# A decoder trunk's head: unused products in TensorE's pauses, x transposed between conditioning bursts, a second job's loads moved ahead

## The chip, the cores and the metric

The kernel runs on one core of a Trainium2 chip. The metric is the device time of one launch in microseconds (us). TensorE (PE in the profile; PEld is its weight load) multiplies and transposes into PSUM, VectorE (DVE), ScalarE (ACT) and GpSimd (POOL) work elementwise, and SyncE (SP) issues most of the transfers.

## What is computed

One layer of a decoder trunk, for a prompt of 256 tokens and for 8 samples of 8 tokens, which share all weights. In the reference (cut):

```python
mod = jax.nn.silu(c) @ w_ada + b_ada
sh1, sc1, g1, sh2, sc2, g2 = jnp.split(mod, 6, axis=-1)
h = _rmsnorm(x, norm1_g) * (1 + sc1) + sh1
p = h @ w_in                      # q, k, v, og, u, ga, gb, alr
o, s_new = _gla(q, k, v, loga, s0)
y_a = _rmsnorm(o, gla_norm_g) * silu(og);  y_b = _pool(u_ext, pos0, w_pool, pool_scale)
x = x + g1 * ((sigmoid(ga) * y_a + sigmoid(gb) * y_b) @ w_o)
h2 = _rmsnorm(x, norm2_g) * (1 + sc2) + sh2
gate, up = jnp.split(h2 @ w_gu, 2, axis=-1)
x = x + g2 * ((silu(gate) * up) @ w_down)
```

x is (320, 2048), c is (9, 2048): one row for the prompt, one for each sample; w_ada is 2048 x 12288, w_in 2048 x 11280. All is float32.

## The kernel before

All activations lie transposed in SBUF: 128 channels on the partitions, the 320 tokens along the free dimension (`TP` 256 of the prompt, then 64 of the samples). The 2048 channels are 16 column blocks, k = 0 to 15.

**Exact products in three.** A piece of weights (`raw`) comes by a transfer that SyncE issues; ScalarE rounds it to `whi` (L152), VectorE takes the rest, `wlo` (L153), and each 128x128 block takes three products in a row (`mm3`, L166 to L168): hh by whi, hl by whi, hh by wlo, where hh and hl are the same split of h. `raw` has three buffers, so the fourth piece of w_in waits until the first has been split.

**The head** (the pool `head`, from the loads of c and x on) prepares h. c is transposed (16 small transposes), its silu goes to `scT`. x comes in three row blocks `xn`; for every column block k three transposes (128, 128 and 64 rows) go into one buffer of the small PSUM pool (`misc`, four buffers), and VectorE or ScalarE copies them out to `xT[k]` (L462). Then the transposes of the bias and gain vectors (`bada`, `vec`), the sums of squares on ScalarE (L476), their square root behind a table load (L477), the reciprocal (L478) and three diagonal matrices `dg` (L483), with which three products (L484) spread 1/rms over all partitions: `rx`.

**Conditioning in jobs.** The modulation is made in slices of column blocks, `SLICES = ((0, 2), (2, 4), (4, 8), (8, 12), (12, 16))`. A `HeadJob` for a slice loads pieces of w_ada (eight buffers, `araw`), multiplies them with scT in bursts over four or two channel blocks (L218; 32 products on TensorE for a job of two blocks), and `finish` copies the sum (L438), transposes it (L129) and adds bias and gain (L233, L236) into `mod`. `h_unit(k)` then makes hh[k] and hl[k] (L490 to L499). The first job runs alone in the head; the job of the next slice is spread between the products of the slice before it.

**Slices of w_in.** For each slice, 15 units (q, k, v in two halves, u, og, ga, gb, and four gb units of other heads) multiply their 256 columns of w_in over the slice's two or four blocks into `pmain` (two PSUM buffers of two banks), and are copied or added out (`evac`, L338 to L355). The slices of two blocks take v, og, ga and gb in pairs (`proj_pair`).

**What sets the order.** The order of instructions on each engine is settled when the kernel is built: a scheduler ranks them by their place in the code and by what they wait for, and an instruction that is handed to `tc.keep_in_program_order` keeps its place among the others so marked on its engine. SyncE issues its transfers in the order of the code and waits in that order for free buffers.

Of the kernel before, what the change touches and what calls it, by code (L numbers as in the profile page):

```python
# [80 lines left out]
def body(tc, A):  # L81
# [74 lines left out]
    def split_chunk(src, nk, nn):  # L156
# [13 lines left out]
    def proj(w, col, k0, k1, xh, xl):  # L170

        ps = pmain.tile([P, 2, 512], F32, tag="pm", name=nm("ps"))
        for c0 in range(k0, k1, 4):
            nk = min(4, k1 - c0)
            for j, whi, wlo in split_chunk(w[:, c0:c0 + nk, col:col + 256], nk, 256):
# [21 lines left out]
    def proj_pair(w, col, k0, k1, xh, xl):  # L197

        parts = list(split_chunk(w[:, k0:k1, col:col + 512], k1 - k0, 512))
# [179 lines left out]
    with tc.tile_pool(name="head", bufs=1) as xp:  # L379
# [17 lines left out]
        nc.gpsimd.dma_start(vr1[64:68, :], A["gla_norm_g"][0].rearrange("(r p) -> r p", p=P))  # L397
        pt = misc()
# [4 lines left out]
        S.activation(csig, crT, AF.Sigmoid)  # L403
# [5 lines left out]
        class HeadJob:  # L409
# [25 lines left out]
            def finish(self):  # L435
                nb = self.s // 2
                sb = xp.tile([P, 2 * P], F32, tag="adasb", name=nm("adasb"))
                S.copy(sb[:, 0:self.w], self.ps[:, 0:self.w])  # L438
                pt = misc()
                for c in range(nb):  # L440
                    tr(pt[:, c * P:(c + 1) * P], sb[:, c * P:(c + 1) * P])
# [11 lines left out]
        for k in range(KT):  # L453
# [4 lines left out]
            if k < SLICES[0][1]:  # L458
                xT.append(xp.tile([P, T], F32, name="xT%d" % k))
            else:  # L460
                xT.append(hp.tile([P, T], F32, tag="hl%d" % k, name="xT%d" % k))
            (S.copy if k % 2 else V.tensor_copy)(xT[k], pt[:, 0:T])  # L462

        pt = misc()
# [7 lines left out]
        ssq = xp.tile([P, 3], F32, name="ssq")  # L472
        V.memset(ssq, 1.0)
        for i in range(3):
            n = P if i < 2 else TS
            S.activation(junk[:n], xn[i][:n], AF.Square, accum_out=ssq[:n, i:i + 1])  # L476
# [3 lines left out]
        dg = xp.tile([P, 3, P], F32, name="dg")  # L480
        for i in range(3):
            n = P if i < 2 else TS
            V.tensor_scalar(dg[:n, i, :n], ident[:n, :n], ssq[:n, i:i + 1], None, op0=ALU.mult)  # L483
            PE.matmul(prs[:, i * P:i * P + n], lhsT=ones[:n, :], rhs=dg[:n, i, :n], start=True, stop=True)  # L484
        rx = xp.tile([P, T], F32, name="rx")
        V.tensor_copy(rx, prs[:, 0:T])
# [42 lines left out]
        for f in HeadJob(0, SLICES[0][1]).steps():  # L529
            f()  # L530
        for k in range(SLICES[0][1]):
            h_unit(k)
        for si, (k0, k1) in enumerate(SLICES):
            bg = []
            acc = 0 if si == 0 else 1
            if si + 1 < len(SLICES):
# [5 lines left out]
                bg += HeadJob(n0, n1 - n0).steps()  # L542
# [673 lines left out]
```

## Time and profile before

| | |
|---|---|
| time of the kernel before, median of 3 runs | 1988.42 us (1988.23 to 1989.18) |
| the profiled execution's own time | 1986.94 us |
| its span from the first to the last instruction | 1985.1 us |
| TensorE busy, mean granted clock over the span | 98%, 0.993 |
| VectorE, ScalarE, GpSimd busy | 51%, 41%, 7% |
| transfers | 400.84 MB, mean 202 GB/s |

Times within the profile count from the span's start; the span is 1.8 us shorter than the execution's own time. A matmul's duration contains its way through the array, so successive products overlap, and their spacing is what a product costs.

### The profile page before, as it was taken

What the parts mean: (1) busy time and instruction counts of PE and PEld (TensorE: products, weight loads), DVE (VectorE), ACT (ScalarE), POOL (GpSimd) and SP (SyncE); (2) the same over time, 40 slices, a digit from 0 to 9 for tenths busy, and PEclk for the clock granted to TensorE, in tenths of its full rate; (3) what the DMA queues carried; (4) which work ended last, traced back from release to release, by engine and by line L of the source; (5) the groups of instructions that cost most, each with busy time, mean ns of one, the idle gap of its engine ahead of it and who ended that gap; (6) DMA issues with size and microseconds to landing.
All of it is one profiled execution on the core that took longest, in us unless ns stands there. A gap on an engine that the chain in (4) does not pass through costs nothing.

```text
span 1985.1 us, 37225 instructions
## 1 busy us (share of the span) xinstructions
PE 1943.5 (98%) x15030; PEld 1850.1 (93%) x15030; DVE 1012.2 (51%) x1888; ACT 818.8 (41%) x1470; POOL 135.6 (7%) x259
## 2 busy tenths in 40 slices
PE   7999999999999999999999999999999999999997
PEld 5789998898999899888999999999999999999997
DVE  2556565474546544664474434444444444444554
ACT  4333374354336433643354333333333434344443
POOL 1112220111010100110030000000000000000000
PEclk9999999999999999999999999999999999999998
DMA  9888754775975787579656666444445444444443
GB/s 299 288 303 271 228 168 141 266 267 181 329 249 167 279 273 232 168 252 331 223 156 219 198 217 195 142 153 146 151 145 159 149 149 149 150 151 146 149 141 93
DMA packets 324607, 400.84 MB, mean 202 GB/s; under 512 B 13545, under 2 KB 264681, under 8 KB 324097
## 3 DMA queue, kind: packets, MB, share of 16 engines
q1 hardware_dynamic: 312162, 358.21, 56.2%
q0 software_dynamic: 12272, 40.25, 5.5%
q8 instruction: 118, 1.93, 0.4%
q14 instruction: 55, 0.45, 0.1%
HBM read 373.96 MB, written 24.67 MB: 201 GB/s over the span
## 4 chain that ended last, share of the span: by engine, by line
PE 91%; DMA 5%; DVE 2%; ACT 1%; issue 0%; SPq 0%; DVEq 0%; ACTq 0%
PE ps L166 27%; PE ps L168 26%; PE ps L167 26%; PE pm L218 4%; DMA raw<-w_in 2%; PE pm L129 2%; DMA raw<-w_ada 1%; DMA raw<-w_o 1%; PE pm L804 1%; PE pm L825 1%; PE pm L773 1%; DVE wlo L153 1%; DMA xn<-x_sample 1%; DMA x<-xspill 0%; PE pm L800 0%
## 5 line engine op out<-in xcount | busy, mean ns | idle before, releaser
L153 DVE TENSOR_TENSOR wlo<-raw,whi 128x512 fp32r<-128x512 f32 x953 | 658.8, 696 | 813.1 <-ACT whi L152 809.9
L152 ACT CAST whi<-raw 128x512 fp32r<-128x512 f32 x953 | 586.2, 621 | 987.0 <-PE ps L167 825.8
L166 PE MATMUL ps<-hh,whi 128*128 128x320 f32 x1408 | 443.2, 315 | 6.0 <-ACT hh L495 2.7
L168 PE MATMUL ps<-hh,wlo 128*128 128x320 f32 x1408 | 440.3, 313 | 0.4 <-DVE wlo L153 0.2
L167 PE MATMUL ps<-hl,whi 128*128 128x320 f32 x1408 | 438.6, 312 | 0.3 <-DVE hl L499 0.3
L166 PE MATMUL ps<-h2h,whi 128*128 128x320 f32 x1408 | 437.3, 311 | 1.4 <-ACT h2h L1100 1.4
L167 PE MATMUL ps<-h2l,whi 128*128 128x320 f32 x1408 | 436.2, 310 | 0.5 <-DVE h2l L1086 0.5
L168 PE MATMUL ps<-h2h,wlo 128*128 128x320 f32 x1408 | 436.0, 310 | 0.0
L166 PEld LDWEIGHTS ps<-hh,whi 128*128 128x128 f32 x1408 | 265.3, 188 | 24.9 <-issue 10.5
L168 PEld LDWEIGHTS ps<-hh,wlo 128*128 128x128 f32 x1408 | 265.5, 189 | 8.6 <-issue 5.7
L167 PEld LDWEIGHTS ps<-hl,whi 128*128 128x128 f32 x1408 | 265.6, 189 | 7.5 <-issue 5.9
L166 PEld LDWEIGHTS ps<-h2h,whi 128*128 128x128 f32 x1408 | 265.0, 188 | 3.8 <-issue 2.2
L167 PEld LDWEIGHTS ps<-h2l,whi 128*128 128x128 f32 x1408 | 265.3, 188 | 0.9 <-DVE h2l L1086 0.9
L168 PEld LDWEIGHTS ps<-h2h,wlo 128*128 128x128 f32 x1408 | 265.2, 188 | 0.0
L166 PE MATMUL ps<-ah,whi 128*128 128x320 f32 x704 | 218.5, 310 | 0.0
L168 PE MATMUL ps<-ah,wlo 128*128 128x320 f32 x704 | 217.7, 309 | 0.0
L167 PE MATMUL ps<-al,whi 128*128 128x320 f32 x704 | 217.6, 309 | 0.0
L167 PEld LDWEIGHTS ps<-al,whi 128*128 128x128 f32 x704 | 132.2, 188 | 0.0
L166 PEld LDWEIGHTS ps<-ah,whi 128*128 128x128 f32 x704 | 132.2, 188 | 0.0
L168 PEld LDWEIGHTS ps<-ah,wlo 128*128 128x128 f32 x704 | 132.1, 188 | 0.0
L218 PE MATMUL pm<-raw,scT 128*32 128x128 f32 (+1 forms) x2688 | 103.0, 293 | 4.7 <-DMA raw<-w_ada 4.7
L218 PEld LDWEIGHTS pm<-raw,scT 128*32 128x32 f32 x2688 | 70.7, 110 | 25.5 <-issue 13.8
(292 smaller groups left out, 1540.2 us busy)
## 6 DMA issues: line engine op xcount, KB each, us to landing
raw<-w_ada SPq DMA_DIRECT2D x192, 512.0 KB, 6.1
raw<-w_gu SPq DMA_DIRECT2D x176, 512.0 KB, 3.5
raw<-w_in SPq DMA_DIRECT2D x173, 512.0 KB, 4.4
raw<-w_down SPq DMA_DIRECT2D x79, 512.0 KB, 3.3
S<-state_gla POOLq DMA_DIRECT2D x16, 1024.0 KB, 8.5
o_gs<-S POOLq DMA_DIRECT2D x16, 1024.0 KB, 7.6
raw<-w_o SPq DMA_DIRECT2D x32, 512.0 KB, 5.1
raw<-w_down SPq DMA_DIRECT2D x15, 256.0 KB, 2.6
```

Of the source, the lines that this page charges most:

```text
L129: PE.transpose(out, in_, ident[:k, :k])
L152: S.copy(hi, raw)
L153: V.tensor_sub(lo, raw, hi.bitcast(F32))
L166: PE.matmul(ps, lhsT=whi, rhs=xhi, start=start, stop=False)
L167: PE.matmul(ps, lhsT=whi, rhs=xlo, start=False, stop=False)
L168: PE.matmul(ps, lhsT=wlo, rhs=xhi, start=False, stop=stop)
L218: ins = PE.matmul(ps[32 * j:32 * j + 32, 0:w], lhsT=scT[:, k, :], rhs=raws[j], start=k == 0 if start is None else start, stop=k == KT - 1 ...
L773: PE.matmul(pt, lhsT=E["kdn"][:, s, d * P:(d + 1) * P], rhs=E["vn"][:, s], start=s == 0, stop=s == 1)
L804: PE.matmul(pt[32 * j:32 * j + 32, :], lhsT=qeP[:, d, 4 * gg + j, :], rhs=E["S0", gg, d][:, j], start=False, stop=d == 1, tile_position=(0 ...
L825: PE.matmul(pt, lhsT=kpz[:, gg, j, d * P:(d + 1) * P], rhs=E["vp"][:, gg], start=True, stop=True)
```

## The change

**Unused products.** A tile `fill` (128x512, ones) is made by four copies on VectorE, and `keep_busy(n)` multiplies it n times into a PSUM buffer that nobody reads. It is called with 6 ahead of c's transposes, 3 behind them; 9, 6 and 3 behind the transposes of x's first, second and third row block; 4 after the transposes behind each of the first three bursts; 1 before and 6 after `finish`.

**x between bursts.** Only column blocks 0 to 2 are transposed as x's row blocks land. The other 13 follow in program order behind the first job's bursts: 4, 5, 4 and none. The sums of squares come ahead of that, and the norm (`x_norm`) ahead of the third burst; it also leaves the normalized x of blocks 0 and 1 ready, to which `h_first` applies the modulation.

**Loads and splits.** The second job's first four pieces of w_ada (`job1.load(0)`, `job1.load(4)`) are issued ahead of w_in's fourth piece (unit u). The splits of w_in's first four pieces (`EarlySplit`) and `h_first` stand in one fixed order on ScalarE and VectorE.

The core of the diff:

```diff
+    class EarlySplit:
...
+        def hi(self):
+            tc.keep_in_program_order(S.copy(self.h, self.raw))
+
+        def lo(self):
+            tc.keep_in_program_order(V.tensor_sub(self.l, self.raw, self.h.bitcast(F32)))
...
+        def keep_busy(n):
+
+            for _ in range(n):
+                tc.keep_in_program_order(PE.matmul(idle[:, 0, :], lhsT=fill[:, 0:P], rhs=fill, start=True, stop=True))
...
+        keep_busy(6)
         pt = misc()
         for k in range(KT):
-            tr(pt[:, 16 * k:16 * k + 9], crow[:, k * P:(k + 1) * P])
+            ptr(pt[:, 16 * k:16 * k + 9], crow[:, k * P:(k + 1) * P])
+        keep_busy(3)
...
+        def x_trans(k, eng):
             pt = misc()
             for i in range(3):
                 n = P if i < 2 else TS
-                tr(pt[:, i * P:i * P + n], xn[i][:n, k * P:(k + 1) * P])
...
+                ptr(pt[:, i * P:i * P + n], xn[i][:n, k * P:(k + 1) * P])
+            xT.append(x_place(k))
+            (S.copy if eng else V.tensor_copy)(xT[k], pt[:, 0:T])
+
+        job0 = HeadJob(0, SLICES[0][1])
+        for k0 in range(0, KT, 4):
+            job0.load(k0)
...
+        for i in range(3):
+            n = P if i < 2 else TS
+            S.activation(junk[:n], xn[i][:n], AF.Square, accum_out=ssq[:n, i:i + 1])
+        pts = [misc() for _ in range(NX0)]
+        for i in range(3):
+            n = P if i < 2 else TS
+            for k in range(NX0):
+                ptr(pts[k][:, i * P:i * P + n], xn[i][:n, k * P:(k + 1) * P])
+            keep_busy((9, 6, 3)[i])
+        for k in range(NX0):
+            xT.append(x_place(k))
+            V.tensor_copy(xT[k], pts[k][:, 0:T])
...
+        def x_norm():
+            dg = xp.tile([P, 3, P], F32, name="dg")
+            for i in range(3):
+                n = P if i < 2 else TS
+                V.tensor_scalar(dg[:n, i, :n], ident[:n, :n], ssq[:n, i:i + 1], None, op0=ALU.mult)
+                tc.keep_in_program_order(PE.matmul(prs[:, i * P:i * P + n], lhsT=ones[:n, :], rhs=dg[:n, i, :n],
+                                                   start=True, stop=True))
+            V.tensor_copy(rx, prs[:, 0:T])
+            for k in range(SLICES[0][1]):
+                t = xp.tile([P, T], F32, tag="xh", bufs=2, name=nm("xh"))
+                V.tensor_tensor(t, xT[k], rx, op=ALU.mult)
+                xhat.append(t)
+
+        def h_first(k):
+
+            t = xhat[k]
+            E = G if k else V
+            pinned(S.activation(hh[k][:, 0:TP], t[:, 0:TP], AF.Identity, scale=modp(1, k), bias=modp(0, k)))
+            pinned(E.tensor_tensor(s3(t[:, TP:T]), s3(t[:, TP:T]), mods(1, k), op=ALU.mult))
+            pinned(E.tensor_tensor(s3(t[:, TP:T]), s3(t[:, TP:T]), mods(0, k), op=ALU.add))
+            pinned(S.copy(hh[k][:, TP:T], t[:, TP:T]))
+            hl[k] = hp.tile([P, T], F32R, tag="hl%d" % k, name="hl%d" % k)
+            pinned(V.tensor_scalar(t[:, 0:TP], t[:, 0:TP], modp(1, k), modp(0, k), op0=ALU.mult, op1=ALU.add))
+            pinned(V.tensor_sub(hl[k], t, hh[k].bitcast(F32)))
...
-        for f in HeadJob(0, SLICES[0][1]).steps():
-            f()
-        for k in range(SLICES[0][1]):
-            h_unit(k)
+        nx = SLICES[0][1]
+        for i, k0 in enumerate(range(0, KT, 4)):
+            if i == 2:
+                x_norm()
+            job0.burst(k0)
+            while len(xT) < (7, 12, 16, 16)[i]:
+                x_trans(len(xT), len(xT) % 2)
+            if i < 3:
+                keep_busy(4)
+        ew = []
+        job1 = HeadJob(nx, SLICES[1][1] - nx)
+        for kind, i, col in units(0)[:5]:
+            if kind == "v" and i == 1:
+                continue
+            if kind == "u":
+                job1.load(0)
+                job1.load(4)
+            raw = raw_chunk(win[:, 0:nx, col:col + (512 if kind == "v" else 256)], nx, 512 if kind == "v" else 256)
+            ready[col] = [EarlySplit(raw)] if kind != "v" else [EarlySplit(raw[:, j:j + 1]) for j in range(nx)]
+            ew += ready[col]
+        keep_busy(1)
+        job0.finish()
+        keep_busy(6)
+        ew[0].hi()
+        h_first(0)
+        ew[0].lo()
+        ew[1].hi()
+        h_first(1)
+        ew[1].lo()
+        for e in ew[2:]:
+            e.hi()
+            e.lo()
```

Where the instructions stand. VectorE, from the silu of c on, before (pm_159 and the like are x's transposes in PSUM, one for each column block):

```order
L404 TENSOR_TENSOR scT<-pm_139,csig 128x16x9
L462 COPY xT_163<-pm_159 128x320
L462 COPY xT_175<-pm_171 128x320
L462 COPY xT_187<-pm_183 128x320
L462 COPY xT_199<-pm_195 128x320
L478 RECIPROCAL ssq<-ssq 128x3
L483 TENSOR_SCALAR dg<-cst,ssq 128x128 x2
L483 TENSOR_SCALAR dg<-cst,ssq 64x64
```

And the same engine and place in the changed kernel (pm_195, pm_196 and pm_197 are column blocks 0 to 2):

```order
L445 TENSOR_TENSOR scT<-pm_151,csig 128x16x9
L538 RECIPROCAL ssq<-ssq 128x3
L547 TENSOR_SCALAR dg<-cst,ssq 128x128 x2
L547 TENSOR_SCALAR dg<-cst,ssq 64x64
L528 COPY xT_225<-pm_195 128x320
L528 COPY xT_227<-pm_196 128x320
L528 COPY xT_229<-pm_197 128x320
```

The reciprocal and dg, which wait for ScalarE's square root, now stand ahead of the first copy of x; four copies stood ahead of them.

TensorE in the changed kernel, from x's second row block to burst 0 (pm_247 is the first job's sum, pm_231 the vectors' transposes; in brackets the semaphores that a row waits for, of which DVE_49 is VectorE's):

```order
L431 MATMUL idle_139<-fill 128x512 x6
L435 MATMUL pm_195<-cst,xn_122 128x64 [waits DMAHW4_49]
L435 MATMUL pm_196<-cst,xn_122 128x64
L435 MATMUL pm_197<-cst,xn_122 128x64
L431 MATMUL idle_139<-fill 128x512 x3
L129 MATMUL pm_231<-cst,vr_133 128x68 [waits DMASW4_49,DMASW3_49,DMASW5_49,DMASW2_49,DMASW1_49]
L242 MATMUL pm_247<-raw_174,scT 32x128 [waits DMAHW5_49,DVE_49]
L242 MATMUL pm_247<-raw_174,scT 32x128
```

Burst 0 (pm_247) stood behind all transposes of x and the norm; now it stands behind those of three column blocks, and the other blocks follow it.

SyncE's queue before, from w_in's first piece on (raw_393 to raw_479 of w_in are the pieces of q, k, v and u):

```order
L142 DMA raw_393<-w_in 128x2x256
L142 DMA raw_413<-w_in 128x2x256
L142 DMA raw_436<-w_in 128x2x512
L142 DMA raw_474<-w_ada 128x4x256
L142 DMA raw_476<-w_ada 128x4x256
L142 DMA raw_479<-w_in 128x2x256
```

And in the changed kernel:

```order
L142 DMA raw_414<-w_in 128x2x256
L142 DMA raw_418<-w_in 128x2x256
L142 DMA raw_422<-w_in 128x2x512
L142 DMA raw_428<-w_ada 128x4x256
L142 DMA raw_430<-w_ada 128x4x256
L142 DMA raw_432<-w_ada 128x4x256
L142 DMA raw_434<-w_ada 128x4x256
L142 DMA raw_436<-w_in 128x2x256
```

Two more pieces of the second job stand ahead of u's.

## Rows read from the trace of the kernel before

**Rows 1.** Page, part 1: busy us, share of the span, instructions, by engine.
```profile
PE 1943.5 (98%) x15030; PEld 1850.1 (93%) x15030; DVE 1012.2 (51%) x1888; ACT 818.8 (41%) x1470; POOL 135.6 (7%) x259
```

**Rows 2.** Busy time by stretch; columns: from:to, length, then as its header says.
```profile
core 0: us, PE busy (x) PEld busy (x) DVE busy (x) ACT busy (x) POOL busy (x), PEclk, DMA share, GB/s
13.71:24.67 10.96, 10.96 (x36) 5.64 (x36) 4.02 (x11) 5.46 (x11) 0.00 (x0) 1.00 1.10 350
...
34.86:40.59 5.73, 5.40 (x24) 4.75 (x25) 2.12 (x6) 1.85 (x5) 3.24 (x7) 0.70 1.05 333
...
50.00:75.00 25.00, 25.00 (x252) 23.07 (x251) 16.07 (x29) 10.78 (x21) 5.11 (x10) 1.00 0.79 258
75.00:95.00 20.00, 17.22 (x155) 12.61 (x152) 8.13 (x13) 4.15 (x8) 0.00 (x0) 1.00 1.00 363
```

**Rows 3.** Chain of waits, 26 to 41 us; columns: start, length, engine, tile, line.
```profile
29.99 1.52 PE pm L218 x48
...
32.51 0.19 DVE mod L236
...
40.59 0.41 PE ps L166
```

**Rows 4.** Timeline of ScalarE, 12.9 to 33.2; start, length, operation.
```profile
14.85 1.22 ACT L462 COPY xT<-pm 128x320 f32<-128x320 f32 x3
16.09 1.28 ACT L477 ACT_TABLE_LOAD   x1
17.39 0.30 ACT L477 ACTIVATE ssq<-ssq,epst 128x3 f32<-128x3 f32 x1
```

**Rows 5.** Timeline of VectorE, 13 to 36.5.
```profile
17.71 0.18 DVE L478 RECIPROCAL ssq<-ssq 128x3 f32<-128x3 f32 x1 [0.66 <-ACT ssq L477]
18.00 0.64 DVE L483 TENSOR_SCALAR dg<-cst,ssq 128x128 f32<-128x128 f32 x3
18.56 0.48 DVE L462 COPY xT<-pm 128x320 f32<-128x320 f32 x1
...
33.57 1.51 DVE L153 TENSOR_TENSOR wlo<-raw,whi 128x512 fp32r<-128x512 f32 x2
...
35.68 0.47 DVE L497 SCALAR_TENSOR_TENSOR hl<-xh,mod,hh 128x256 fp32r<-128x256 f32 x1
```

**Rows 6.** Transposes by line L129: ns min/median/max, first and last start us.
```profile
L129 PE MATMUL pm<-cst,w x56: 270/272/415, 324.9 to 822.1; 128*128 128x128 f32 x56
...
L129 PE MATMUL pm<-cst,xn x48: 311/418/477, 6.8 to 24.4; 128*128 128x128 f32 x32, 64*128 64x64 f32 x16
```

**Rows 7.** Timeline of TensorE, 6 to 39.3.
```profile
24.89 1.73 PE L484 MATMUL pm<-dg,cst 128*128 128x128 f32 x6
...
34.86 0.68 PE L166 MATMUL ps<-hh,whi 128*128 128x320 f32 x2 [2.68 <-ACT hh L495]
...
36.77 0.47 PE L167 MATMUL ps<-hl,whi 128*128 128x320 f32 x1
37.04 0.47 PE L168 MATMUL ps<-hh,wlo 128*128 128x320 f32 x1
...
38.90 0.31 PE L167 MATMUL ps<-hl,whi 128*128 128x320 f32 x1
39.05 0.31 PE L168 MATMUL ps<-hh,wlo 128*128 128x320 f32 x1
```

**Rows 8.** Conditioning products of the first job, line L218, columns as in rows 6.
```profile
L218 PE MATMUL pm<-raw,scT x128: 272/273/421, 26.6 to 31.2; 128*32 128x128 f32 x128
```

**Rows 9.** Busy time from 26 to 30 us, columns as in rows 2.
```profile
26.00:30.00 4.00, 4.00 (x88) 3.48 (x91) 0.49 (x1) 0.38 (x1) 0.32 (x1) 1.00 0.18 51
```

**Rows 10.** Page, part 6: DMA issues, count, KB each, median us to landing.
```profile
raw<-w_in SPq DMA_DIRECT2D x173, 512.0 KB, 4.4
```

**Rows 11.** Busy time of three later stretches, columns as in rows 2.
```profile
612.00:615.10 3.10, 3.10 (x27) 3.09 (x27) 2.73 (x10) 1.31 (x3) 0.00 (x0) 1.00 0.23 41
275.00:280.00 5.00, 3.64 (x24) 3.18 (x22) 3.15 (x5) 4.97 (x9) 1.55 (x1) 1.00 0.21 71
280.00:285.00 5.00, 4.98 (x21) 4.77 (x22) 3.56 (x6) 4.90 (x9) 0.09 (x1) 0.66 0.68 195
```

More of the change, by code (lines that the diff above doesn't have):

```diff
@@ L154, in split, with __init__, split_chunk @@
         return hi, lo
-    def split_chunk(src, nk, nn):
+    ready = {}
+    class EarlySplit:
+        def __init__(self, raw):
+            n = raw.shape[2]
+            self.raw = raw
+            self.h = wp.tile([P, 512 // n, n], F32R, tag="whi", bufs=WB, name=nm("whi"))
+            self.l = wp.tile([P, 512 // n, n], F32R, tag="wlo", bufs=WB, name=nm("wlo"))
+        def hi(self):
+            tc.keep_in_program_order(S.copy(self.h, self.raw))
+        def lo(self):
+            tc.keep_in_program_order(V.tensor_sub(self.l, self.raw, self.h.bitcast(F32)))
+    def split_chunk(src, nk, nn, key=None):
+        if key in ready:
+            k = 0
+            for e in ready.pop(key):
+                for j in range(e.h.shape[1]):
+                    yield k, e.h[:, j], e.l[:, j]
+                    k += 1
+            return
         raw = raw_chunk(src, nk, nn)
@@ L174, in proj @@
             nk = min(4, k1 - c0)
-            for j, whi, wlo in split_chunk(w[:, c0:c0 + nk, col:col + 256], nk, 256):
+            for j, whi, wlo in split_chunk(w[:, c0:c0 + nk, col:col + 256], nk, 256, col if w is win else None):
                 kt = c0 + j
@@ L397, in body, with ptr @@
         nc.gpsimd.dma_start(vr1[64:68, :], A["gla_norm_g"][0].rearrange("(r p) -> r p", p=P))
+        idle = pmain.tile([P, 2, 512], F32, tag="pm", name=nm("idle"))
+        fill = xp.tile([P, 512], F32R, name="fill")
+        V.tensor_copy(fill[:, 0:P], ones)
+        for c in range(1, 4):
+            V.tensor_copy(fill[:, c * P:(c + 1) * P], ones)
+        def keep_busy(n):
+            for _ in range(n):
+                tc.keep_in_program_order(PE.matmul(idle[:, 0, :], lhsT=fill[:, 0:P], rhs=fill, start=True, stop=True))
+        def ptr(out, in_):
+            k = in_.shape[0]
+            tc.keep_in_program_order(PE.transpose(out, in_, ident[:k, :k]))
+        keep_busy(6)
         pt = misc()
         for k in range(KT):
-            tr(pt[:, 16 * k:16 * k + 9], crow[:, k * P:(k + 1) * P])
+            ptr(pt[:, 16 * k:16 * k + 9], crow[:, k * P:(k + 1) * P])
+        keep_busy(3)
         csig = xp.tile([P, KT, 9], F32, name="csig")
         crT = pt[:, 0:256].rearrange("p (k r) -> p k r", r=16)[:, :, 0:9]
-        S.activation(csig, crT, AF.Sigmoid)
+        tc.keep_in_program_order(S.activation(csig, crT, AF.Sigmoid))
         V.tensor_tensor(scT[:, :, 0:9], crT, csig, op=ALU.mult)
@@ L437, in finish @@
                 sb = xp.tile([P, 2 * P], F32, tag="adasb", name=nm("adasb"))
-                S.copy(sb[:, 0:self.w], self.ps[:, 0:self.w])
+                ins = S.copy(sb[:, 0:self.w], self.ps[:, 0:self.w])
+                if self.b0 == 0:
+                    pinned(ins)
                 pt = misc()
                 for c in range(nb):
-                    tr(pt[:, c * P:(c + 1) * P], sb[:, c * P:(c + 1) * P])
+                    (tr if self.b0 else ptr)(pt[:, c * P:(c + 1) * P], sb[:, c * P:(c + 1) * P])
                 src = pt[:, 0:nb * P].rearrange("p (c j r) -> p j c r", j=4, r=32)
@@ L452, in body, with x_place @@
         xT = []
-        for k in range(KT):
+        NX0 = 3
+        def x_place(k):
+            if k < SLICES[0][1]:
+                return xp.tile([P, T], F32, name="xT%d" % k)
+            return hp.tile([P, T], F32, tag="hl%d" % k, name="xT%d" % k)
+        def x_trans(k, eng):
             pt = misc()
@@ L456, in body @@
                 n = P if i < 2 else TS
-                tr(pt[:, i * P:i * P + n], xn[i][:n, k * P:(k + 1) * P])
[L458 to L462, printed above, removed]
+                ptr(pt[:, i * P:i * P + n], xn[i][:n, k * P:(k + 1) * P])
[4 more added lines that the diff above has]
+            job0.load(k0)
+        ssq = xp.tile([P, 3], F32, name="ssq")
+        V.memset(ssq, 1.0)
+        for i in range(3):
[10 more added lines that the diff above has]
+            V.tensor_copy(xT[k], pts[k][:, 0:T])
         pt = misc()
@@ L479, in body @@
         prs = misc()
[L480 to L484, printed above, removed]
-        rx = xp.tile([P, T], F32, name="rx")
-        V.tensor_copy(rx, prs[:, 0:T])
+        rx = xp.tile([P, T], F32, name="rx")
+        xhat = []
+        def x_norm():
[20 more added lines that the diff above has]
+            pinned(V.tensor_sub(hl[k], t, hh[k].bitcast(F32)))
         def h_unit(k):
```

9 lines of the change are left out of this document (2 added, 7 removed).

## The prediction

> **What bounds the kernel now.** I began with the page: TensorE is busy for 98% of the span [rows 1], so a change pays only where TensorE stands still, waits for transfers, or runs at half its clock. Then the busy time by stretch [rows 2]. Read it from the end of the head: from 50 to 75 us TensorE is busy 25.00 of 25.00 us, so what the head gains or loses before that is carried to the end; from 75 to 95 us it loses 2.8 us to loads (DMA share 1.00). So the question is when the first job's results are ready and when the products of w_in run densely. The chain of waits gives both marks [rows 3]: the last conditioning product ends at 31.51, the modulation is ready at 32.70, and the first product of unit v starts at 40.59. I call the first mark E and the last V; V - E is 9.08 us before.
>
> Two things fill that head. Ahead of E stand 36 transposes of x in one stretch of 10.96 us [rows 2], then the norm's products, then four bursts of the first job. Behind E stand the chain through VectorE, and 24 products of q and k, of which the first start 0.27 us apart and later ones 0.15 us [rows 7]: the granted clock is 0.70 over 34.86 to 40.59 [rows 2], 1.2 GHz in its first part and 2.4 GHz after.
>
> **The clock ahead of E.** The views print a granted clock of 1.00 from 13.71 on, but the durations say otherwise: a transpose of x takes 418 ns (median), one of the same 128x128 form later 272 ns [rows 6]; the conditioning products range from 421 down to 272 ns [rows 8]. I read the transposes of x, the norm and the first half of the bursts as 1.2 GHz, with the record of the clock beginning only after the rise. What TensorE did matters: 11 us of transposes without a pause left the clock at 1.2 GHz; the norm's products and the bursts behind them raised it. The Trainium skill (TensorE: Matmul & The Clock Gate, Part 4: PE-mode transpose) says that the full clock does not engage for transposes, since they don't count as busy in the same way; this trace agrees with its 418 ns. Taken strictly, that rule speaks against mixing transposes among the bursts: it is the half-clock rival below, 1997.6 us, against the 1991.8 that I forecast.
>
> **The change, part by part.**
> 1. *When burst 0 can start.* PSUM's small pool has four buffers: the transposed conditioning vector's and three of x's first transposes fill them, the gain and bias vectors' transposes take over the first one, so the job's own accumulator takes that of x's column block 0, and waits until VectorE has copied it out. In VectorE's new order that copy stands behind the reciprocal and the three dg operations, which wait for ScalarE's square root. On ScalarE the third square ends at 14.85, where three copies of x (1.22 us) stood before the table load [rows 4]; they are gone. So: 14.85, plus table load to square root 1.30 (16.09 to 17.39), square root to reciprocal 0.32 (to 17.71), reciprocal to dg 0.29 (to 18.00), dg to the next copy 0.56 (to 18.56), plus that copy 0.48 [rows 4, 5], gives 17.8. Before, this queue cost nothing: copies of x ran ahead of the reciprocal. TensorE gets there at about the same time even at 1.2 GHz: 27 unused products of 512 columns at 0.43 us (0.27 us for 320 columns, scaled; 0.24 at 2.4 GHz from 0.15 [rows 7]) are 11.6 us of the time from about 2.5 us on. They cost nothing by themselves, being covered by the waits for x and for this copy; without that cover they would cost 11.6 us at 1.2 GHz and 6.5 at 2.4.
> 2. *From burst 0 to E.* The row of work is now: 4 bursts, 13 column blocks of x (three transposes each), 12 unused products, the norm. Prices at 2.4 GHz: a burst of 32 products 1.01 us (48 take 1.52 [rows 3]); a block 0.59 us (10.96 / 12 = 0.91 at 1.2 GHz, times 272 / 418); an unused product 0.24; the norm 1.12 (1.73 [rows 7] times 272 / 421). Sum 4.0 + 7.7 + 2.9 + 1.1 = 15.7 us. At 1.2 GHz: bursts 1.56 each (1.01 times 421 / 272), blocks 0.91, products 0.43, norm 1.73: 6.2 + 11.9 + 5.2 + 1.7 = 25.0 us. So E lies between 17.8 + 15.7 = 33.5 and 42.8, against 31.51. Even at full clock E is later, because 13 of 16 blocks now stand behind a burst that starts at 17.8, where they ran from 13.71.
>  I take the middle way that the trace points at: products at 2.4 GHz, transposes at 1.2. That is 4.0 + 11.9 + 2.9 + 1.1 = 19.9, E = 37.7. It is nearest to the row of 11 us of transposes; a dense run of transposes between products, from 612 to 615.1 us, kept a granted clock of 1.00, but the mere wait of 1.4 us in 275 to 280 us was followed by a fall, mean 0.66 over the next 5 us [rows 11]. So the clock can go either way in each gap.
> 3. *From E to V.* The modulation is again 1.19 us behind E [rows 3]. Normalized x is ready ahead, the sums of w_in's first two pieces need only one split each, and q's first product waits for hh at about E + 2.1, where it was 3.35. VectorE then sets the pace: small operations and the wait for hh to about E + 2.1 (0.18 each for the like [rows 5], ScalarE between them), hl 0.59 (0.47 for 256 columns), wlo 0.75, the in-place update 0.25, hl 0.59, wlo 0.75, two more wlo 1.51 [rows 5]: 6.5, and I take 6.3 since some waits overlap. The 24 products need 3.6 us at 2.4 GHz and fit. The gain on 9.08 is 2.8 us, of which the clock is half. The six unused products behind the job's last transpose lie in that wait and cost nothing.
> 4. *Transfers.* Before, the queues were nearly empty from 26 to 30 us (DMA share 0.18 [rows 9]); now four pieces of the second job follow at once, released by bursts 0 and 1. But w_in's fourth piece (unit u) stands behind them and waits for the first wlo, E + 3.5. It is needed after 24 products of v, at E + 6.3 + 3.6; the like land 4.4 us after their issue (median) [rows 10], so 2 us of cover remain. The next pair of w_ada and the piece for og queue behind it: 1.75 MB and 0.64 MB of spilled x at the 363 GB/s of [rows 2] are 6.6 us, so og is in SBUF near E + 12, and TensorE asks for it at E + 12.7, after 36 products and a burst. That is even: bounds 0 and 1 us, I take 0.
> 5. *fill's four copies, the fixed order on ScalarE and POOL*: a fraction of a microsecond at 2 us, ahead of x's landing; nothing.
>
> **Sum.** V = 37.7 + 6.3 = 44.0 against 40.59: +3.4 us. The profiled execution took 1986.94 us, so 1990.3; the median of the runs is 1988.42, 1.48 above it, and on that scale I forecast 1991.8 us. A measurement of this kernel can tell about 0.2%, 4.0 us, from no change.
>
> **Rivals.**
> - *Full clock throughout* (25%): the unused products hold 2.4 GHz across the transposes, as in 612 to 615.1. V = 33.5 + 6.3 = 39.8, -0.8 us: 1987.6. Against it: the gaps with four or five blocks hold mostly transposes.
> - *Half clock nearly throughout* (17%), the slower side: the wait for the copy at 17.8 drops the clock and transposes keep it down. E = 42.8, and the 24 products at 0.27 us add 0.7: V = 49.8, +9.2, less if a burst raises it: up to 1997.6. It decides from about E = 38.3, where the loss passes 4 us.
> - *The transfers pay* (9%), the faster side: the idle of 2.8 us at 75 to 95 shrinks because pieces run ahead, on top of full clock: 1987.6 - 2.8 = 1984.8. Against it: later pieces are still released by TensorE's and VectorE's progress, so the loads move with the head and don't get ahead of it.
> - *The change doesn't do what it says*: bursts and transposes run in the given order, but the second job's early pieces only wait in SBUF. That is inside the forecast; alone it moves nothing.
> - *Forecast* (43%): 1991.8, its own range 1989.4 to 1994.5. The remaining 6% lie beyond both ends.
>
> From these: faster by over 0.2% 0.08 (half of the transfers' case and some of the rest); within 0.2% 0.54 (full clock, two thirds of the forecast's range); slower 0.38 (a third of it, and the half-clock case). The range takes in full clock and most of the half-clock case: 1985.8 to 1997.0.
>
> **What would show it.** Step 1: the first burst starts at 17.5 to 18.5, released by VectorE's copy of block 0. Step 2: E at 33 to 43, and the spacing of three transposes of a block (0.59 or 0.91 us) says which case; low clock in the records ahead of E would confirm it. Step 3: V - E near 6.3, no low clock in q and k. Step 4: no empty queue at 27 to 30, a new one before u's piece. The prediction is wrong if burst 0 starts at the landing of its pieces, or if blocks cost well under 0.59 us.

## The result, and the profile after

Five runs of the changed kernel gave a median of 1995.48 us (1992.13 to 1999.57), five of the kernel before beside them 1988.42 (1986.40 to 1989.18): ratio 1.0039, 95% interval 1.0027 to 1.0050. The change makes the kernel slower, by 7.1 us in this set. The profiled execution of the changed kernel is the slowest of its five (1999.57 us, span 1997.8); that of before took 1986.94. So the two profiles lie 12.6 us apart, more than the medians. A second set of five runs of the changed kernel (experiment 9) has a median of 1997.38 against 1987.98, 9.4 us slower: 1.0040, 1.0028 to 1.0052.

The page of the changed kernel, part 1, and its busy time by stretch, columns as in [rows 1, 2]:

```profile
PE 1956.5 (98%) x15076; PEld 1858.6 (93%) x15076; DVE 1013.9 (51%) x1895; ACT 817.9 (41%) x1469; POOL 133.9 (7%) x255
```

```profile
13.71:24.67 10.96, 7.08 (x54) 4.11 (x52) 2.96 (x12) 5.08 (x8) 0.00 (x0) 0.66 1.10 349
34.86:40.59 5.73, 5.73 (x53) 3.59 (x51) 1.88 (x8) 2.42 (x7) 0.65 (x3) 1.00 0.01 3
50.00:75.00 25.00, 25.00 (x268) 23.43 (x267) 15.99 (x31) 13.46 (x25) 5.12 (x10) 1.00 0.82 276
75.00:95.00 20.00, 17.38 (x156) 13.38 (x158) 7.91 (x13) 1.76 (x3) 0.00 (x0) 1.00 0.96 326
```

From 13.71 to 24.67 TensorE was busy all the time before; now it stands still for 3.88 of 10.96 us. From 34.86 to 40.59 the transfers, at 333 GB/s before, are at 3: the gap in the queues of [rows 9] has not gone, it has moved to here. Between 50 and 75 us TensorE is as full as before, so what the head loses is carried on.

TensorE's timeline of the changed kernel (start, length, operation, idle time before it and what ended it):

```profile
15.31 0.22 PE L129 MATMUL pm<-cst,vr 68*128 68x68 f32 x1
19.41 1.94 PE L242 MATMUL pm<-raw,scT 128*32 128x128 f32 x32 [3.88 <-DVE xT L528]
21.28 3.73 PE L435 MATMUL pm<-cst,xn 128*128 128x128 f32 x12
24.94 2.07 PE L431 MATMUL idle<-fill 128*128 128x512 f32 x4
26.94 1.36 PE L242 MATMUL pm<-raw,scT 128*32 128x128 f32 x32
28.23 2.92 PE L435 MATMUL pm<-cst,xn 128*128 128x128 f32 x15
37.44 1.08 PE L242 MATMUL pm<-raw,scT 128*32 128x128 f32 x32
```

Burst 0 waits 3.88 us for VectorE's copy. Behind this pause TensorE runs at the lower clock: burst 0 takes 1.94 us, and four column blocks of x take 3.73 us, 0.92 from one to the next, the price at which [rows 6] has 418 ns for a transpose. The clock's records have 0.50 from 17.3 to 27.6 us and 1.00 behind, and the next five blocks, transposes like the ones before them, take 2.92 us, 0.57 from one to the next. The last burst ends at 38.52: mark E, 7.0 us later than before.

VectorE's timeline says why burst 0 waits, ScalarE's why VectorE does; the counterpart of [rows 4, 5]:

```profile
18.04 0.18 DVE L538 RECIPROCAL ssq<-ssq 128x3 f32<-128x3 f32 x1 [10.47 <-ACT ssq L537]
18.32 0.64 DVE L547 TENSOR_SCALAR dg<-cst,ssq 128x128 f32<-128x128 f32 x3
18.88 1.27 DVE L528 COPY xT<-pm 128x320 f32<-128x320 f32 x3
```

```profile
14.39 1.91 ACT L519 ACTIVATE junk<-xn 64x2048 f32<-64x2048 f32 x1
16.41 1.28 ACT L537 ACT_TABLE_LOAD   x1
17.71 0.30 ACT L537 ACTIVATE ssq<-ssq,epst 128x3 f32<-128x3 f32 x1
```

VectorE has been idle for 10.47 us when the square root comes; the copies, whose data were in PSUM since 14.6, stand behind it.

The chain of waits behind E, the counterpart of [rows 3] (start, length, what):

```profile
39.60 0.19 DVE mod L260
...
42.13 4.55 DMA raw<-w_in
46.71 0.62 ACT whi L168
47.33 0.61 ACT k L377
47.99 0.42 PE ps L190
```

The modulation is ready 1.27 us behind E (1.19 before). V, the 25th product, starts at 45.33: V - E is 6.81 us, 2.3 less than the 9.08 before. Then a new wait follows: u's piece of w_in, issued at 31.20 before and so ahead of E, is issued at 42.13, 3.6 us behind E, and lands 4.55 us later; then ScalarE splits it, and k's evacuation, which stands behind that split in ScalarE's order, holds TensorE's 37th product to 47.99. The evacuations of slice 0 from 61.95 us on (before) come 5.48 us later: +7.01 at E, -2.27 on the way to V, +0.74 by this wait.

### The profile page after: what moved, and what is told of

It is laid out like the page before. It is cut to its first block, busy times and chain, and to the rows that moved or that the text cites. A ratio compares the mean times of both kernels' runs of the same rounds, so it can differ in the third digit from the quotient of the medians.

```text
span 1997.8 us, 37323 instructions
## 1 busy us (share of the span) xinstructions
PE 1956.5 (98%) x15076; PEld 1858.6 (93%) x15076; DVE 1013.9 (51%) x1895; ACT 817.9 (41%) x1469; POOL 133.9 (7%) x255
## 3 DMA queue, kind: packets, MB, share of 16 engines
HBM read 373.96 MB, written 24.67 MB: 200 GB/s over the span
## 4 chain that ended last, share of the span: by engine, by line
PE 91%; DMA 5%; DVE 1%; ACT 1%; issue 0%; SPq 0%; DVEq 0%; ACTq 0%
PE ps L190 27%; PE ps L192 26%; PE ps L191 26%; PE pm L242 4%; DMA raw<-w_in 2%; DMA raw<-w_ada 2%; PE pm L129 1%; PE pm L912 1%; PE pm L933 1%; PE pm L881 1%; DMA xn<-x_prompt 1%; DMA raw<-w_o 0%; PE pm L435 0%; DVE wlo L153 0%; PE pm L908 0%
```

## The experiments

All were run beside the kernel before, in three groups; its medians there were 1988.58, 1987.98 and 1989.58. "Slice 0" is how much later than in the profile of before the evacuations from 61.95 us on come; "profile" how much longer the profiled execution took than that of before. E, V - E, slice 0 and "profile" come from one execution of each kernel, the median and its ratio from 5 to 12. E of before is the end of the chain's piece in [rows 3]; read from the timeline like the others it is 31.44 and V - E 9.15. One profile is one execution out of a spread: the runs of experiments 1 and 2 reach from 1982.77 to 1996.19 and from 1981.58 to 1996.18, those of before beside them from 1985.11 to 1991.32.

| | E | V - E | slice 0 | profile | median us | ratio, 95% |
|---|---|---|---|---|---|---|
| before | 31.51 | 9.08 | 0 | 0 | 1988.42 | |
| changed | 38.52 | 6.81 | +5.5 | +12.6 | 1995.48 | 1.0027 to 1.0050 |
| 9 changed, again | 38.40 | 6.82 | +5.4 | +11.5 | 1997.38 | 1.0028 to 1.0052 |
| 1 copies first | 32.51 | 6.82 | -0.9 | +3.6 | 1988.97 | 0.9992 to 1.0016 |
| 2 no products | 34.45 | 9.29 | +3.0 | +2.7 | 1989.51 | 0.9991 to 1.0016 |
| 3 x first | 33.58 | 10.18 | +3.0 | +3.4 | 1989.03 | 0.9992 to 1.0009 |
| 4 u first | 37.32 | 6.82 | +11.4 | +9.9 | 1999.92 | 1.0058 to 1.0094 |
| 5 none between bursts | 28.48 | 6.82 | -4.9 | -5.4 | 1981.97 | 0.9953 to 0.9977 |
| 6 splits early | 31.32 | 10.29 | +3.4 | +11.9 | 1991.77 | 1.0013 to 1.0037 |
| 7 x first, splits early | 32.24 | 8.06 | +6.4 | +8.5 | 1992.54 | 1.0009 to 1.0027 |
| 10 changed, none between | 38.73 | 7.02 | +6.1 | +8.6 | 1990.60 | 0.9995 to 1.0020 |
| 11 pure delay | 37.16 | 6.81 | +4.2 | +2.2 | 1993.91 | 1.0009 to 1.0028 |
| 12 one split early | 28.18 | 8.02 | -4.5 | +0.7 | 1982.99 | 0.9962 to 0.9983 |
| 13 none at the end | 28.47 | 8.35 | -2.8 | -1.4 | 1983.59 | 0.9961 to 0.9983 |

My theory (1): E comes late because burst 0 waits for copies that stand behind the square root, because the pause drops the clock, and because 13 blocks stand behind that burst. The rivals: (2) the unused products cost TensorE's time; (3) the moved loads decide.

**1. The copies first.** VectorE's three copies pinned ahead of the reciprocal.

```diff
-            V.tensor_copy(xT[k], pts[k][:, 0:T])
+            pinned(V.tensor_copy(xT[k], pts[k][:, 0:T]))
-        V.reciprocal(ssq, ssq)
+        pinned(V.reciprocal(ssq, ssq))
```

> The changed kernel with one thing moved on VectorE: the three copies of x's first blocks out of PSUM (xT, L528) stand ahead of the reciprocal and of dg, which wait for ScalarE's square root; TensorE's order and the loads stay. Theory 1 (burst 0 is held by these copies behind the reciprocal; the 3.9 us pause of TensorE drops its clock; the rest of the delay is 13 blocks of transposes behind burst 0): burst 0 starts at 15.5 to 16.5 us instead of 19.41, TensorE's pause ahead of it is under 1 us, the transposes behind it take 0.575 us a block and the bursts 1.08 us from the start, mark E comes at 33 to 35.5 instead of 38.45, time 3 to 5 us under the changed kernel's. Theory 2 (the unused products cost): burst 0 comes earlier but E moves by less than 1.5 us, time within 2 us of the changed kernel's. Theory 3 (the moved loads decide): E moves as in theory 1, but the evacuations of slice 0 and the time move by less than 2 us.

VectorE's timeline, then TensorE's:

```profile
12.84 1.29 DVE L528 COPY xT<-pm 128x320 f32<-128x320 f32 x3 [5.95 <-PE pm L435]
16.21 0.18 DVE L538 RECIPROCAL ssq<-ssq 128x3 f32<-128x3 f32 x1 [1.63 <-ACT ssq L537]
```

```profile
13.92 0.41 PE L242 MATMUL pm<-raw,scT 128*32 128x128 f32 x4
15.32 1.90 PE L242 MATMUL pm<-raw,scT 128*32 128x128 f32 x28 [0.99 <-DMA raw<-w_ada]
17.15 2.99 PE L435 MATMUL pm<-cst,xn 128*128 128x128 f32 x12
```

Burst 0 starts at 13.92, the pause of 3.88 us is gone and one of 0.99, for w_ada, stands in its place. E is 6.0 us earlier and so is slice 0 (5.48 + 0.88 = 6.4); the median goes back to that of before, 0.4 us above it where the changed kernel's are 7.1 and 9.4. One order on VectorE is worth 6.4 us of slice 0 and 6.7 or more of the median. Theory 1 holds in that; by theory 2 E would hardly have moved, by theory 3 slice 0. It was not right throughout: burst 0 came before the expected 15.5, E 0.5 us before the expected range, the gain passed the expected 5 us, and the clock did not hold. Its record has 0.50 from 15.4 to 18.8 us, so the 28 products behind the shorter pause took 1.90 us, where the same 28 take 1.07 in experiment 11.

**2. No unused products**, on top of experiment 1 (`for _ in range(0)` in keep_busy).

> The kernel of e1 without the unused products (keep_busy issues none); the transposes of x between the bursts, the early pieces of w_in and the loads stay. Theory 1: without the products TensorE's clock is at its lower level until TensorE has worked through the first transposes, so burst 0 at 15.5 to 16.5, blocks of 0.92 us and bursts of 1.9 us over most of the stretch, minus some 4.5 us of products: E at 34 to 37, time 0 to 2 us over that of e1. Theory 2 (the products cost their own time): E comes 3 to 4.5 us earlier than in e1 and the time is 3 us or more under e1's.

TensorE's timeline of this kernel:

```profile
17.15 3.73 PE L435 MATMUL pm<-cst,xn 128*128 128x128 f32 x12
...
22.67 4.64 PE L435 MATMUL pm<-cst,xn 128*128 128x128 f32 x15
...
30.87 2.57 PE L435 MATMUL pm<-cst,xn 128*128 128x128 f32 x12
```

All blocks to 27 us take 0.92 us: TensorE works without a pause from 15.3 on, and stays at 1.2 GHz until 31, where the last four blocks begin and the clock's first record of 1.00 stands (31.3). E is 1.9 us later than in experiment 1 although the products, 3.3 us by their starts, are gone. V moved more, since the scheduler now put u's split ahead of q's evacuation. The times of 1 and 2 can't be told apart, so taken all together the products gain nothing that these runs can show.

**3. All of x ahead of the bursts**, as in the kernel before, without unused products.

```diff
-        for i, k0 in enumerate(range(0, KT, 4)):
-            if i == 2:
-                x_norm()
+        while len(xT) < KT:
+            x_trans(len(xT), len(xT) % 2)
+        x_norm()
+        for k0 in range(0, KT, 4):
             job0.burst(k0)
```

> No unused products, and all transposes of x and its norm ahead of the four bursts as in the kernel before; the early pieces of w_in, ScalarE's and VectorE's fixed order behind the last burst and the second job's loads stay as in the change. Theory 1: the transposes fill the time in which w_ada lands, E is at 31 to 32.5 (31.51 before); V minus E stays at 6 to 7.5 us (9.08 before), so V is 1 to 2.5 us earlier than before, and the time is 0.5 to 2.5 us under the kernel before's. Theory 3 (the moved loads cost): E and V as said, but the time stays at or over that of the kernel before, with u's piece or a later piece of w_in waited for.

TensorE's timeline, then ScalarE's:

```profile
14.38 11.95 PE L435 MATMUL pm<-cst,xn 128*128 128x128 f32 x39
```

```profile
42.48 0.62 ACT L168 CAST whi<-raw 128x512 fp32r<-128x512 f32 x1 [4.64 <-DMA raw<-w_in]
43.01 0.70 ACT L377 ACTIVATE q<-ps 128x640 f32<-128x640 f32 x1
```

E came 1.1 us outside the expected range, and V - E, expected at 6 to 7.5, took 10.18: ScalarE waits 4.64 us for u's piece with q's evacuation behind it. So the new chain alone gains nothing here: its order on ScalarE has to fit the landing of that piece. The time is that of before.

**4. u's piece ahead of the second job's loads.** The two job1.load calls, four pieces of w_ada (the expectation says eight), behind raw_chunk. None of the second job's pieces then stands ahead of u's, where the kernel before had two and the changed kernel has four; so this is not the order of before, as the expectation's "again" has it.

> The changed kernel with the loads of the second job (eight pieces of w_ada) behind u's piece of w_in again, in place of ahead of it. Theory 3 (the order of the loads decides): the time moves by 2 us or more, down if u's late piece (1.94 us of ScalarE, 0.73 us of TensorE) is what costs, up if the second job's late pieces hold og. Theory 1: E stays at 38 to 39, V at 45 to 46, ScalarE's wait for u's piece goes, and the time is within 1.5 us of the changed kernel's, 0 to 1.5 us under it.

ScalarE's timeline:

```profile
45.66 0.62 ACT L168 CAST whi<-raw 128x512 fp32r<-128x512 f32 x1 [2.09 <-DMA raw<-w_in]
...
55.86 1.14 ACT L152 CAST whi<-raw 128x512 fp32r<-128x512 f32 x2 [4.51 <-DMA raw<-w_in]
59.99 2.42 ACT L152 CAST whi<-raw 128x512 fp32r<-128x512 f32 x4 [2.99 <-DMA raw<-w_in]
```

u's wait stays (2.09 us): what holds that piece is its buffer, which the first piece's split frees, not its place in the queue. And og's piece now lands late: slice 0 loses 6 us more, and the median is 11.3 us over that of before, where the changed kernel's are 7.1 and 9.4. So four early pieces are worth 2 to 4 us against none, as theory 3's second half has it; my expectation of a time 0 to 1.5 us lower was wrong. What the change's own step from two to four does was not run.

**5. No products between the bursts**, on top of experiment 1; those ahead of burst 0 and behind burst 3 stay.

```diff
-            if i < 3:
-                keep_busy(4)
```

> The kernel of the first experiment (VectorE's three copies first) without the twelve unused products between the bursts; those ahead of burst 0 and the seven behind burst 3 stay. What holds TensorE's clock up across the transposes of x? Theory P (any dense work holds it once it is up): the blocks stay at 0.575 us, the stretch loses the 3.6 us of the products, E at 28.5 to 29.5 (32.5 with them), V at 35.5 to 37. Theory Q (the products hold it; transposes count for nothing): blocks go back to 0.92 us and bursts to 1.9 us within the stretch, E at 31 to 34.5 (34.45 without any unused product). Time: by theory P 1985 to 1988 us, by theory Q 1988 to 1990 us, since u's piece is waited for in both.

TensorE's timeline of this kernel, then its busy time from 12 us to E, columns as in [rows 2]:

```profile
15.94 1.08 PE L242 MATMUL pm<-raw,scT 128*32 128x128 f32 x32
16.95 2.35 PE L435 MATMUL pm<-cst,xn 128*128 128x128 f32 x12
...
20.25 2.92 PE L435 MATMUL pm<-cst,xn 128*128 128x128 f32 x15
...
27.40 1.08 PE L242 MATMUL pm<-raw,scT 128*32 128x128 f32 x32
```

```profile
12.00:28.48 16.48, 16.48 (x194) 11.22 (x192) 6.83 (x20) 7.43 (x13) 0.00 (x0) 1.00 1.09 353
```

The blocks take 0.57 us throughout, without a product between them. E is 28.48, 4.0 earlier than in experiment 1 (3.3 of it the products' own time), and the time is 1981.97 us, 6.0 under the kernel before and better than both kernels. That is theory P, with a time 3 us under its range of 1985 to 1988. Beside experiment 2 it shows which products matter: with the 27 ahead of burst 0, E comes at 28.48 in place of 34.45 (the seven behind burst 3 come after E); the twelve in between only cost time here, where the clock is up when they start. The median gains 6.4 us on that of experiment 1, slice 0 4.0; the rest is not explained, and the intervals, some 2.4 us to either side, don't exclude chance. Not run was the kernel with these 27 products and all of x ahead of the bursts: whether x between the bursts has a part in the gain is not shown.

**6. Four splits ahead of burst 3**, on top of experiment 1.

```diff
+            if i == 3:
+                early_three()        # q's, k's, v's pieces: whi and wlo
```

> The kernel of the first experiment, and the splits of w_in's first three pieces (four whi, four wlo) ahead of burst 3 in place of between the operations of h; the buffers of w_in are free earlier, so u's piece is issued earlier. If the wait for u's piece and the place of the splits cost what the trace says: u's piece issued at 27 to 31 us (36.12 in the first experiment), no wait of k's evacuation, V minus E at 5 to 6.2 us (6.8), slice 0 another 1.5 to 3 us earlier, time 1985.5 to 1988. Rival: the load stretch at 75 to 130 us takes it back, time 1988 to 1990.

ScalarE's timeline of this kernel:

```profile
40.34 0.62 ACT L152 CAST whi<-raw 128x512 fp32r<-128x512 f32 x1 [5.03 <-DMA raw<-w_in]
40.86 0.70 ACT L377 ACTIVATE q<-ps 128x640 f32<-128x640 f32 x1
```

u's piece was issued at 30.91 and no longer waited for, as expected. But with that the scheduler set og's split ahead of q's evacuation, and ScalarE waits 5.03 us for og's piece: V - E 10.29. The wait was not removed but passed on, and the kernel is slower.

**7. The same with all of x first** (the splits ahead of the bursts, on top of experiment 3).

> The kernel of the third experiment (no unused products, all of x's transposes and the norm ahead of the bursts), and the splits of w_in's first three pieces ahead of the bursts. The third experiment's V came 10.7 us behind E since u's piece, issued when the first piece's buffer came free behind h, held q's evacuation on ScalarE for 4.6 us. If that is the cause: u's piece issued at 27 to 30 us, no such wait, V minus E at 5.5 to 6.5 us, slice 0 1.5 to 3 us ahead of the kernel before (it was 3.0 behind), time 1985 to 1987.5. If the loads later in slice 1 decide: slice 0 earlier as said, but time 1988 to 1990 as in the third experiment.

ScalarE's timeline of this kernel:

```profile
39.02 0.62 ACT L168 CAST whi<-raw 128x512 fp32r<-128x512 f32 x1 [4.09 <-DMA raw<-w_in]
```

Here u's piece was issued at 31.55, not at 27 to 30: its buffer was free, but on SP it stands behind the second job's loads, which the late bursts release at 29.26. The wait stays, a miss of the expectation (which puts V of experiment 3 10.7 us behind E; by the table it is 10.18).

**9. The changed kernel again.**

> The changed kernel, unaltered, for a second profile beside these. The head should repeat: burst 0 at 19 to 20, E at 38 to 39, slice 0 at +5 to +6 us against the kernel before. Open is what follows: if the 5 to 7 us more that the first profile lost between 82 and 130 us belong to the change, they recur and the median stays at 1994 to 1997; if they vary from run to run, this profile shows a different amount, and its time differs by as much.

TensorE's timeline at burst 0, and ScalarE's in slice 1; last the same place in the first profile of the changed kernel:

```profile
18.12 1.94 PE L242 MATMUL pm<-raw,scT 128*32 128x128 f32 x32 [3.72 <-DVE xT L528]
```

```profile
124.88 1.14 ACT L152 CAST whi<-raw 128x512 fp32r<-128x512 f32 x2 [4.63 <-DMA raw<-w_in]
```

```profile
125.00 1.14 ACT L152 CAST whi<-raw 128x512 fp32r<-128x512 f32 x2 [5.93 <-DMA raw<-w_in]
```

The head repeats, with burst 0 0.9 us earlier than expected. What follows does too: in both profiles the split of one piece waits about 5 us at 119 to 125 us (2.26 before, at 114.36), and TensorE's clock falls right after (from 126.5, here from 128.1). Both profiled executions end 11.5 to 12.6 us later than that of before, 6 to 7 more than slice 0. Each is also the slowest of its five runs. Nor does only this kernel lose time there. By the same evacuations, lateness grows from slice 0 to 225 us by 7.7 and 8.1 us in these two profiles, by 4.4, 8.5 and 5.0 in those of experiments 1, 6 and 12, and by 0.2 to 0.4 in those of 2, 3 and 11.

**10. The changed kernel without the twelve products between the bursts**, VectorE's order of the change kept.

> The changed kernel without the twelve unused products between the bursts, with VectorE's order of the change (reciprocal and dg ahead of the copies, written out). It asks what the middle products do when the clock has fallen in the pause ahead of burst 0. If they lift it again: without them bursts at 1.93 us, blocks at 0.92 us and the norm at 1.84 us all the way, burst 0 at 18 to 19.5, E at 39 to 41 (38.45 with them), time 1995 to 1999. If the clock rises by itself, or by the bursts: E at 34.5 to 37, time 1987 to 1993. If the changed kernel's whole loss is the products' own 4.5 us: time 1989 to 1992 with E at 34 to 35.

Busy time of this kernel from burst 0 to E, columns as in [rows 2]:

```profile
17.55:38.73 21.18, 21.18 (x174) 13.07 (x174) 5.53 (x15) 2.98 (x7) 0.00 (x0) 0.50 0.75 248
```

In the profile the clock stays at 1.2 GHz over all 21 us, and E is 38.73. From burst 0 to E it takes 21.18 us, where the changed kernel took 19.11 and 20.28 with the products: what they cost there, 4.2 us by their starts, they gave back and more, with the clock at 2.4 GHz from 27.6 us on. So in the profiles the products between the bursts are no loss to the changed kernel. But the median is only 1.0 us over that of before in its group, where the changed kernel's are 7.1 and 9.4 over, and not at the 1995 to 1999 that the expectation has beside such an E. The twelve runs fall in two groups, six at 1985.95 to 1988.77 and six at 1992.43 to 1995.51; the profile is one of the upper. What the lower ones did was not seen; that the pause did not cost them the clock is a guess.

**11. A pure delay**, on top of experiment 5: keep_busy(38) ahead of burst 3.

> The kernel of the fifth experiment (1981.97 us) with 38 unused products ahead of burst 3: a pure delay of E by 10.3 us, to that of the changed kernel; bursts 0 to 2, the loads that they release and all orders stay. The changed kernel's evacuations are 5.4 us late in slice 0 but 11.5 to 12.5 us late at its end. If lateness of the head alone does that: slice 0 at +5 to +6 us against the kernel before, the end at +9 to +13, time 1994 to 1998. If a delay is only carried along: time 1992 to 1993.5, end and slice 0 alike. If the changed kernel's loss has another cause (its earlier loads, its clock): time under 1990.

The added products in TensorE's timeline:

```profile
27.23 8.92 PE L431 MATMUL idle<-fill 128*128 128x512 f32 x38
```

Slice 0 moves by 9.1 us against experiment 5, the median from 6.0 under the kernel before to 4.3 over it, 10.3 us. A delay of the head is carried to the end about one to one. Its profiled execution, the fastest of its eleven, shows no fall of the clock in slice 1 and ends only 2.2 us behind that of before: the evacuations are 4.4 us late at 225 us and 1.4 at 390, and in between the profile of before has two falls of the clock, of 3.4 us each from 280.9 and 321.9, that this one doesn't have.

**12. One split early**, on top of experiment 5: whi and wlo of q's piece ahead of burst 3.

> The kernel of the fifth experiment, with the split of w_in's first piece alone ahead of burst 3, so that its buffer comes free earlier and u's piece is issued at 27 to 29 us (32.09 there). If u's piece is what holds k's evacuation: that wait (1.55 us of ScalarE, 0.4 us of TensorE) goes, V minus E at 6 to 6.6 us (6.8), slice 0 another 0.4 to 1.2 us earlier, time 1980 to 1982. If a new wait on ScalarE takes its place, as with all four splits early: time 1983 to 1990.

ScalarE's timeline of this kernel:

```profile
34.93 0.62 ACT L168 CAST whi<-raw 128x512 fp32r<-128x512 f32 x1 [2.50 <-DMA raw<-w_in]
35.45 0.70 ACT L377 ACTIVATE q<-ps 128x640 f32<-128x640 f32 x1
```

u's piece is issued 3.2 us earlier (28.90), lands 1.4 us earlier (34.91), and its split now stands ahead of q's evacuation in place of k's: V - E 8.02, slice 0 0.4 us later. The time is that of experiment 5 within the intervals.

**13. No products behind burst 3**, on top of experiment 5; u's split behind k's evacuation.

> The kernel of the fifth experiment without the seven unused products behind burst 3, and with u's split behind k's evacuation so that q's and k's evacuations don't wait for u's piece. If those products hold the clock over the wait for the modulation: a clock of 0.50 in q's or k's products as in the kernel before, products 0.27 us apart in place of 0.15, V 0.5 to 2 us later than with them (35.30), time 1982 to 1985. If the clock holds without them: V at 34.5 to 35.3, time 1980 to 1982.

Busy time of this kernel in the stretch of its low clock, columns as in [rows 2]:

```profile
33.20:36.60 3.40, 3.40 (x14) 3.40 (x14) 1.65 (x3) 0.70 (x1) 0.00 (x0) 0.50 0.96 289
```

The clock falls inside q's and k's products as it did before, V is 36.82, 1.5 us later, and slice 0 2.1 us. In the time that is not told apart: 1983.59, interval 0.9961 to 0.9983.

## Why the prediction was right or wrong

The direction was as forecast, and the time lies within the range, but above the forecast's own range, between it (1991.8) and the half-clock rival (1997.6). That it lies within is in part luck: the second set, 9.4 us over before, would be 1997.8 on the same scale, beyond the range's end at 1997.0. The prediction also held a time within 0.2% of before the likelier (0.54) and gave slower 0.38, where the two parts that it names, a third of 43% and the 17%, make 0.31. By its steps:

- *Step 1, burst 0 at 17.8, held by the copy behind the square root.* Right in mechanism, and shown by experiment 1. Measured 19.41 and 18.12 in two profiles; in the first, x's second half landed 1.5 us later than before. The step's sum has no price for what the pause does to the clock; only the half-clock rival names it (the wait drops the clock), and in the first profile that came true from 17.3 to 27.6 us. The step had TensorE reach burst 0 just as the copy is done, with the unused products filling the wait; they end at 15.5, and 3.9 us of standing still follow.
- *Step 2, 19.9 us from burst 0 to E.* Measured 19.1 and 20.3. That the sum comes out is luck, for its reason is wrong. It split by kind (products at 2.4 GHz, transposes at 1.2); the rows of the first profile split by time: burst 0, four blocks and four products at 1.2 GHz, what stands behind 27.6 at 2.4. A burst at 1.2 GHz took 1.87 us, from its start to that of the blocks behind it, not the 1.56 that the step scaled from the durations of single products. The Trainium skill (TensorE: Matmul & The Clock Gate, Part 4: PE-mode transpose), which says that the full clock does not engage for transposes, fits experiments 2 and 3, where long rows of them stay at 0.92 us a block; it does not fit experiment 5, where blocks take 0.57 us with no product between them. There the measurement decides; [rows 6] had pointed that way already, with 272 ns for the later transposes.
- *Full clock throughout*, the first rival, was said to need the products between the bursts. Experiment 5 shows that it doesn't: there the clock stayed up with the products ahead of burst 0 and no pause behind them. The price of the twelve products was nearly right, 2.9 us against 3.3 by their starts; what was wrong is that they are worth it. Taking them out of experiment 1 gave 4.0 us at E and some 6 us of time.
- *Step 3, V - E 6.3.* Measured 6.81 or 6.82 in six of the profiles with the changed chain; 0.5 us too low.
- *Step 4, the transfers even.* og was right (its piece landed at 51.0, forecast E + 12). u's piece was not: I gave it 2 us of cover by asking when TensorE needs it. ScalarE needs it earlier, since in its fixed order the split stands ahead of k's evacuation: 0.74 us, and in experiments 2, 3, 6, 7 and 12, where a split stands ahead of q's, 1.2 to 3.5 us more between E and V. That the second job's early pieces move nothing alone was not put to the test: experiment 4, with none of them ahead of u's piece, lost 2 to 4 us more, but before had two there.
- *Carried to the end.* Sum of these: +5.5 in slice 0 in place of +3.4. The medians are 7.1 and 9.4 us over before. The delay of experiment 11 was carried about one to one, so 1.6 to 4 us are left, of which the smaller lies within the noise (the first interval reaches from 5.4 to 9.9 us). Both profiles lose more between 75 and 130 us, where a piece of w_in is waited for and the clock falls. It is not the late head that does it, for the profiles of experiments 1 and 12, whose slice 0 is earlier than before, lose 3 to 5 us there as well, and that of experiment 11 loses nothing; why the piece is late in some profiles stays open.

So the change holds a gain of 6 us (experiment 5) and two losses. The copies behind the square root, some 6.5 us, are shown by moving them. The products between the bursts, some 6 us, are shown as a loss only once the copies stand first; with the copies behind (experiment 10) the profile shows none at E, though the median falls by 6 us or more. As the two were taken away one after the other, the sum (6.5 + 6 - 6) makes the 7 us, but it does not say what each costs by itself.

## What to carry to other kernels

Before filling pauses of an engine with unused work, look for the wait that would end the fill: here it was an evacuation queued behind an operation that it does not need, and moving it was worth 6.4 us of slice 0, while all the filling together gained nothing that could be told (experiments 1 and 2). Here filling paid ahead of a row of dense work, where it got the clock up, and not inside the row once the clock was up; behind a pause that had cost the clock (experiment 10 beside the changed kernel) the fill inside gave back its own time. A split or evacuation in a fixed order waits with the slowest of what stands ahead of it: ask not when the last engine needs a transfer, but when the first in-order queue comes to it.

## What the hardware showed

- A row of transposes kept the level at which it was entered: 39 of them took 11.95 us at the lower level (experiment 3), and bursts and blocks without a pause stayed at 1.2 GHz for 21 us (experiment 10), while the same row, entered at 2.4 GHz, kept 2.4 for 12.5 us and beyond (experiment 5). This is what these profiles show, not a rule: in experiment 2 the row of experiment 10 rose to 2.4 GHz after 16 us, with no unused product in it.
- A pause ahead of burst 0 went with the clock: after 2.7 to 3.9 us (changed kernel, experiments 4, 9 and 10) the record has 0.50 for 10 to 24 us, after 0.99 us (experiment 1) for 3.4 us, and after 0.7 us or none (experiments 5, 6, 11 and 12) it stayed at 1.00.
- The granted clock is printed as 1.00 ahead of the first record of a trace: in experiment 2, whose first record stands at 31.3 us, blocks took 0.92 us at a printed 1.00. There only the durations tell.
